# Transposing three quarters of the second branch's attention output by DMA, as 16 bit halves, instead of on TensorE

## The chip, the cores and the metric

The kernel runs on one core of one Trainium2 chip. The metric is the device time of one execution in microseconds (us); the median of three runs of the kernel before is 1930.79 us (1929.85 to 1930.82). A core has five engines that run side by side, each with its own queue in program order: TensorE (PE, with its weight loads as PEld), VectorE (DVE), ScalarE (ACT), GpSimd (POOL) and SyncE (SP). SP computes nothing here; nearly all DMAs are issued from its queue, in order, and 16 DMA engines then move the bytes.

## The reference

One encoder block on a 2048 x 1024 input, in single precision. What matters here, cut to its core:

```python
h = rms_norm(x, norm_gain)
qa, ka, va, qb, kb, vb, ga, gb, mg = split(h @ w_in)
ya = banded_attention(rms(qa), rms(ka), va, 128, ...) * silu(ga)
for g, (window, dilation) in enumerate(((128, 1), (512, 4), (2048, 16))):
    o, l = dilated_group(rms(qb[g]), rms(kb[g]), vb[g], window, dilation, ...)
yb = sum(softmax(lses) * outs) * silu(gb)
x = x + (sigmoid(mg_a) * (ya @ w_branch_a) + sigmoid(mg_b) * (yb @ w_branch_b)) @ w_out
```

The first branch (`ya`, A) and the second (`yb`, B) each give a 2048 x 512 output. The projections that use them want it with features on the partitions, the attention makes it with tokens on the partitions, so all of it has to be transposed once.

## The kernel before

**Stages.** First the input is normalised, transposed and split into two half precision tiles `XH` and `XL` (high and low part). Then comes the attention phase, from about 82 to 1250 us of the span. After it come the remaining gates by a Strassen-like scheme (`fps` tiles, line 1576), the branch projections (1885) and the output projection (1957).

**The attention phase** works through 14 units, in the order A0, B(0,1), A1, B(0,2), B(0,0), B(1,1), B(1,2), B(1,0), B(2,1), ... B(3,0); in B(p,g), p is one of four pairs of heads and g the dilation group. A unit has 8 pairs, and a pair projects two blocks of 128 tokens to queries, keys and values (`Pair`, line 677; matmuls into `pj`, line 694). ACT, DVE and POOL then normalise them and split them into halves (`rw`, `spl`; lines 708 to 776), and a DMA transpose turns each block's queries and keys (`kq<-spl`, line 784). For each block of queries an `Item` (line 788) has logits on TensorE (`s<-kq`, 844), maxima, exponentials and a split on DVE and ACT (859 to 876), a DMA transpose of the probabilities (`pt<-p`, 882) and values on TensorE (`pv<-vt,pt`, 893). Within a pair of heads the unit of group 0 is last: there `b_merge_q` (1024) merges the three groups with what was stored of the other two (`zz<-zd`, 902) into the tile `ya` (1062, 1063), 256 tokens at a time.

**The transpose in question.** Every 512 tokens, when a `ya` tile of 128 tokens x (4 blocks x 128 features) is full, a `YPart(chunk, q, y)` (932) is planned. Chunks 0 to 3 are branch A, chunk 4 + p is head pair p of branch B, and q counts the four 512 token pieces. For branch B it does this: four single precision transposes of 128 x 128 on TensorE into one PSUM bank (`turn`, 957), one copy by ACT to SBUF (`gate`, 962, tile `yo` out of a ring of three), and a store to DRAM (`store`, 974, `ytd<-yo`). The later stages load `ytd`.

**What sets the order.** The attention phase is recorded with a manual schedule: `at(t, f)` puts a step at a logical time on one list, where one unit of t is one pair (some 9.7 us while the group 0 units run), and the steps are written out in the order of t. So each engine's queue, SP's with it, holds its instructions in exactly that order, and a queue whose first instruction waits holds back all behind it. `Y_PART` (69) gives the offsets of a YPart's steps, `B_MERGE` those of the merge, `NORM` (62) those of the normalisation up to the `kq` transpose. The weights of the next unit are loaded 384 KB at a time at the start of a unit (`wraw`, 175), since the offsets are logical, and the last two pairs' `kq` transposes of a unit are issued when the next unit has begun.

Of the kernel before, what the change touches and what calls it, by code (L numbers as in the profile page):

```python
# [21 lines left out]
F32 = mybir.dt.float32  # L22
F16 = mybir.dt.float16
I32 = mybir.dt.int32
AF = mybir.ActivationFunctionType
OP = mybir.AluOpType
AX = mybir.AxisListType
# [38 lines left out]
OUT = 0.007  # L66
A_MERGE = (0.085, 0.224, 0.51, 0.59, 1.398, 0.699)
B_MERGE = (-0.037, 0.133, 0.333, 0.507, 0.665, 0.991)
Y_PART = (-0.02, 0.571, 0.797, 0.981, 1.031)
GATE = (-0.062, 0.084, 0.255)  # L70
W_STEP = (0.1, 0.6, 1.9, 0.445, 4.186, 0.117, 0.301)
# [34 lines left out]
def block_kernel(tc, x, w_units, w_gate, w_mrg, w_out, w_bra, w_brk, gain, qkg, sink, bias_a, bias_b, b_merge, out):  # L106
    nc = tc.nc
    V = nc.vector
    A = nc.scalar
# [14 lines left out]
    def ucol():  # L124

        ucount[0] += 1
        return ubuf[:, ucount[0] - 1:ucount[0]]
# [15 lines left out]
    def pow2(mx, name):  # L143
# [3 lines left out]
        p = sm.tile([128, 1], F32, name="pw_p")  # L147
        V.tensor_scalar(p[:].bitcast(I32), m[:].bitcast(I32), 0x7F800000, None, OP.bitwise_and)
        r = sm.tile([128, 1], F32, name="pw_r")
# [39 lines left out]
    def norm_pow(ps):  # L189
# [5 lines left out]
        p = sm.tile([128, 1], F32, name="pw_p")  # L195
        V.tensor_scalar(p[:].bitcast(I32), m[:].bitcast(I32), -0.5, float(0x5F3759DF), OP.mult, OP.add)
        V.tensor_scalar(p[:].bitcast(I32), p[:].bitcast(I32), 0x7F800000, None, OP.bitwise_and)
        s = ucol()
# [5 lines left out]
    def w_square(u, i):  # L204
# [4 lines left out]
        c = slice(2 * i, 2 * i + 2)  # L209
        A.activation(wtiles[u][2][:, c, :n], raw[:, c, :n], AF.Square, accum_out=wtiles[u][3][:, i:i + 1])  # L210

# [11 lines left out]
    def w_hi(u, i):  # L223
        n = 384 if u < NU else 256
        raw, s, inv, wh, wl = wtiles[u]
        c = slice(2 * i, 2 * i + 2)
        A.activation(wh[:, c, :n], raw[:, c, :n], AF.Copy, scale=s[:])

# [20 lines left out]
    def rs_guess(a, n):  # L249

        y = sm.tile([128, 10], F32, name="rs_y")
        A.activation(y[:, :n], a, AF.Ln)
        A.activation(y[:, :n], y[:, :n], AF.Exp, scale=-0.5)
        return y[:, :n]
# [25 lines left out]
    gp = gps.enter_context(tc.tile_pool(name="gp", bufs=1, side="right"))  # L280
# [33 lines left out]
    def g_square(c):  # L314
        gh = sp0.tile([128, NCH, 128], F16, name="gh", bufs=2)
        gl = sp0.tile([128, NCH, 128], F16, name="gl", bufs=2)
        sq = sm.tile([128, 1], F32, name="gsq")
        A.activation(gh[:], gw[c][0], AF.Square, accum_out=sq[:])
        gw[c] += [gh, gl, sq]
# [11 lines left out]
    def g_hi(c):  # L331
        gh, gl, ih, raw, s = gw[c]
        A.activation(gh[:], raw, AF.Copy, scale=s[:])

# [45 lines left out]
    def at(t, f, *args):  # L380
        seq[0] += 1
        heapq.heappush(heap, (t, seq[0], f, args))
# [8 lines left out]
    def chain(steps):  # L391

        steps = sorted(steps, key=lambda e: e[0])
        done = [0]

        def go(k):
            if done[0] < k or steps[k][1](*steps[k][2:]) is False:
                at(now[0] + .04, go, k)
            else:
                done[0] = k + 1  # L400

        for k, e in enumerate(steps):
            at(e[0], go, k)
# [141 lines left out]
    n = 0  # L545
    for k in X_LD:
        for i in range(4 if k == "u" else 1):
            f, args = {"g": (gain_load, ()), "u": (w_load, (0, (i,)))}.get(k, (x_load, (k,)))
            if k in ("w0", "w1"):
                f, args = g_load, (int(k[1]),)  # L550
# [126 lines left out]
    class Pair:  # L677
# [21 lines left out]
        def plan(self, e):  # L699

            for i in range(2):
                for d, f in zip(EVAC, (self.evac_qk, self.v_hi, self.v_lo)):
                    at(e[i] + d, f, i)
            steps = (self.square, self.stats, self.newton, self.scale, self.gain, self.hi, self.lo, self.swap, self.turn)
            for d, f in zip(NORM, steps):
                at(e[1] + d, f)
# [225 lines left out]
    class YPart:  # L932
# [5 lines left out]
        def load(self):  # L938
# [3 lines left out]
            assert ("gt", self.chunk, self.q) in done  # L942
            nc.sync.dma_start(out=self.o[:], in_=gtd[self.chunk][:, 512 * self.q:512 * self.q + 512])

        def plan(self, t):
            steps = [(t + d, f) for d, f in zip(Y_PART, (self.load, self.turn, self.gate, self.top, self.store))]
            if self.q == 3 and self.chunk < 2:
                steps += [(t + Y_PART[3] + d, f) for d, f in zip(Y_MAX, (self.max1, self.max2, self.max3))]
            chain(steps)
# [74 lines left out]
    def b_merge_q(t, un, zz, q):  # L1024
# [33 lines left out]
        def sums():  # L1058
# [5 lines left out]
            if q % 2:  # L1064
                YPart(4 + j, q // 2, un.y).plan(t + B_MERGE[5])

        for d, f in zip(B_MERGE, (collect, exponents, exps, factors, products, sums)):
            at(t + d, f)
# [135 lines left out]
    for u in range(NU + 1):  # L1204
        t = 8 * u
# [8 lines left out]
    for k in range(8):  # L1214
        u = 3 + k
        t = 8 * u
# [10 lines left out]
    t = 0  # L1227
# [644 lines left out]
    class Branch(Seven):  # L1872
        n, mm_us = 7, MM1
# [65 lines left out]
    class Out(Seven):  # L1939
        n, mm_us = 7, MM  # L1940
# [52 lines left out]
    for s in range(8):  # L1993
        p = pos[0]
# [92 lines left out]
```

## Time and profile before

| | |
|---|---|
| median of 3 runs | 1930.79 us |
| the profiled execution | 1929.74 us, span 1927.9 us |
| granted TensorE clock | 0.998 of full speed |
| DMA transposes `pt<-p` and `kq<-spl` | 256 and 224 |
| TensorE transposes on line 957 | 128, 64 of them for branch B |

The span is what lies between the first and the last recorded instruction; the 1.8 us beside it are start and end. In a timeline row the columns are start, duration (both us), engine (a q marks its queue, which issues DMAs or waits), line, operation, tiles written<-read, form and count, and in brackets the idle time ahead of it with what ended it. Matmuls are pipelined, so the distance between two starts, not the duration, is what one costs the queue.

### The profile page before, as it was taken

The numbers are of one execution on the slowest core, as the hardware profiler recorded it, in microseconds if no ns is written. First come the engines' busy times: TensorE is split into PE (matmuls) and PEld (weight loads), VectorE is DVE, ScalarE is ACT, GpSimd is POOL, SyncE is SP. The second block draws the span as 40 slices with busy tenths as digits, with TensorE's granted clock in tenths as the row PEclk, the third lists the DMA queues.
The fourth block names the chain that finished last, engine by engine and source line by source line (L and its number), as shares of the span: only waits on it lengthen the run. The fifth ranks groups of instructions, "written<-read, shape, count | busy, mean of one in ns | idle before, by whom it ended". The sixth has DMA issues, their size and how long they took to land.

```text
span 1927.9 us, 51082 instructions
## 1 busy us (share of the span) xinstructions
PE 1875.8 (97%) x19242; PEld 1439.0 (75%) x19242; DVE 1505.6 (78%) x3835; ACT 1251.6 (65%) x3015; POOL 578.0 (30%) x1363
## 2 busy tenths in 40 slices
PE   6999999999999999999999999899999999999998
PEld 4568987789999899989999898444444446776774
DVE  7679878986887888888888888658778754987885
ACT  8477768886777777777766766565575775433441
POOL 1034343443453435543455445200000001232121
PEclk9999999999999999999999999999999999999999
DMA  6259998987878679878888677666565568854541
GB/s 254 82 103 194 169 187 138 195 167 156 169 147 181 151 147 201 149 159 173 147 171 161 133 151 152 169 243 206 181 203 172 171 195 269 275 158 123 148 147 68
DMA packets 643447, 326.21 MB, mean 169 GB/s; under 512 B 459264, under 2 KB 598144, under 8 KB 640768
## 3 DMA queue, kind: packets, MB, share of 16 engines
q1 hardware_dynamic: 643056, 322.70, 71.6%
q8 instruction: 150, 2.46, 0.6%
q14 instruction: 97, 0.79, 0.1%
q10 hardware_dynamic: 144, 0.26, 0.0%
HBM read 139.08 MB, written 73.66 MB: 110 GB/s over the span
## 4 chain that ended last, share of the span: by engine, by line
PE 87%; DMA 5%; DVE 4%; ACT 2%; issue 1%; POOL 0%; SPq 0%; DVEq 0%; POOLq 0%
PE pj L694 42%; PE fps L1576 17%; PE fps L1957 7%; PE fps L1885 6%; PE s L844 5%; PE pv L893 4%; DMA pt<-p 2%; PE pj L349 2%; PE pj L301 1%; DMA kq<-spl 1%; PE fps L301 1%; DVE y L1734 1%; PE pt L957 1%; PE s L479 0%; DMA bigl<-sd 0%
## 5 line engine op out<-in xcount | busy, mean ns | idle before, releaser
L694 PE MATMUL pj<-wl,XH 128*128 128x128 f16 (+2 forms) x2816 | 715.2, 268 | 0.0
L694 PE MATMUL pj<-wh,XL 128*128 128x128 f16 (+2 forms) x2816 | 711.6, 269 | 0.0
L694 PE MATMUL pj<-wh,XH 128*128 128x128 f16 (+2 forms) x2816 | 708.6, 268 | 0.0
L694 PEld LDWEIGHTS <-XH 128*128 128x128 f16 x5632 | 575.0, 112 | 54.1
L694 PEld LDWEIGHTS <-XL 128*128 128x128 f16 x2816 | 315.8, 112 | 23.8
L859 DVE CUSTOM_DVE_ANT_0 pr<-s,b,ubuf 128x256 f32<-128x256 f32 (+3 forms) x512 | 219.0, 465 | 44.9 <-PE s L844 42.2
L876 DVE SCALAR_TENSOR_TENSOR p<-pr,p 128x512 f16<-128x512 f32 (+2 forms) x256 | 195.8, 765 | 50.6 <-ACT p L872 48.9
L761 POOL TENSOR_TENSOR rw<-rw,g 128x128 f32<-128x128 f32 (+1 forms) x224 | 149.1, 685 | 202.7 <-DVE rw L754 182.4
L1895 POOL TENSOR_TENSOR g<-g,t 128x512 f32<-128x512 f32 x32 | 48.4, 1514 | 536.6 <-DMA g<-mgd 391.8
L1576 PEld LDWEIGHTS <-wh 128*128 128x128 f16 x1064 | 104.3, 99 | 131.9 <-issue 6.7
L712 ACT ACTIVATE rw<-pj 128x256 f32<-128x256 f32 (+1 forms) x224 | 87.5, 390 | 137.8 <-PE pj L694 137.2
L776 POOL COPY spl<-spl 128x256 f16<-128x256 f16 (+1 forms) x224 | 96.5, 460 | 247.7 <-DVE spl L771 247.7
L872 ACT ACTIVATE p<-pr 128x512 f16<-128x512 f32 (+2 forms) x256 | 157.7, 616 | 15.1 <-DMA pt<-p 10.5
L1885 PE MATMUL fps<-y,bigh 128*128 128x128 f16 x1792 | 153.7, 219 | 2.8 <-DVE r L1818 2.8
L844 PE MATMUL s<-kq 128*128 128x128 f16 (+1 forms) x1856 | 148.4, 218 | 6.7 <-DMA kq<-spl 5.8
L1957 PE MATMUL fps<-WO,mf 128*128 128x512 f16 x672 | 150.3, 379 | 2.4 <-DVE xr L1964 2.4
L1885 PE MATMUL fps<-y,bigl 128*128 128x128 f16 x896 | 151.8, 219 | 0.0
L844 PEld LDWEIGHTS <-kq 128*128 128x128 f16 x2016 | 131.1, 98 | 22.9 <-issue 7.7
L1885 PEld LDWEIGHTS <-bigh 128*128 128x128 f16 x1792 | 139.1, 98 | 10.5 <-issue 3.2
L893 PE MATMUL pv<-vt,pt 128*128 128x65 f16 (+1 forms) x2784 | 131.6, 193 | 8.8 <-DMA pt<-p 8.0
L893 PEld LDWEIGHTS <-pt 128*128 128x128 f16 x3024 | 119.2, 97 | 25.0 <-DMA pt<-p 12.5
L767 ACT ACTIVATE spl<-rw 128x512 f16<-128x512 f32 (+1 forms) x112 | 72.1, 643 | 79.5 <-POOL vt L723 74.0
(250 smaller groups left out, 3823.5 us busy)
## 6 DMA issues: line engine op xcount, KB each, us to landing
wraw<-in_w_units_dram SPq DMA_DIRECT2D x56, 384.0 KB, 4.7
g<-mgd SPq DMA_DIRECT2D x64, 256.0 KB, 5.0
wraw<-in_w_mrg_dram SPq DMA_DIRECT2D x45, 256.0 KB, 5.0
mgd<-t SPq DMA_DIRECT2D x43, 256.0 KB, 3.0
zd<-z SPq DMA_DIRECT2D x128, 66.0 KB, 2.0
zz<-zd SPq DMA_DIRECT2D x64, 132.0 KB, 3.4
xt<-in_x_dram SPq DMA_DIRECT2D x16, 512.0 KB, 7.9
ytd<-yo SPq DMA_DIRECT2D x32, 256.0 KB, 3.3
```

The lines of the kernel that those rows point to most:

```text
L694: out.append(lambda lhs=lhs, rhs=rhs, ch=ch, a=a, b=b, k=k: T.matmul(ps[:, a:b], lhsT=lhs[:, ch, :], rhs=rhs[:, ch, a:b], start=(k == 0), ...
L712: A.activation(self.rw[:, n * i:n * i + n], self.ps[i][:, :n], AF.Copy)
L761: G.tensor_tensor(q[:, i, :un.nq, :], q[:, i, :un.nq, :], g, OP.mult)
L776: G.tensor_copy(sp[:, i, nh:, :, :], sp[:, i, nq:nh, ::-1, :])
L844: T.matmul(self.sv[j][:, o:o + k1 - k0], lhsT=q[:, h, :], rhs=kt[:, un.nq + kh + v * un.nk, k0:k1], start=(v == 0), stop=(v == 1))
L859: V.tensor_tensor_reduce(out=self.pv[:, j, self.p0:self.p0 + W], in0=self.sv[j], in1=un.bias[:, self.h0 + j, self.b0:self.b0 + W], scale=I ...
L872: A.activation(self.sp[:, :128 * n], self.pr, AF.Copy, scale=PSC)
L876: V.scalar_tensor_tensor(self.sp[:, 128 * n:], self.pr, PSC, self.sp[:, :128 * n], OP.mult, OP.subtract)
L893: T.matmul(self.po[:, j, :w], lhsT=p[:, n * j + s, :], rhs=un.v[key][:, vh, c0:c0 + w], start=(k == 0 and s == 0), stop=(k == 2 and s == n ...
L1576: T.matmul(b[k][:], lhsT=w[:, i, ch, :], rhs=xform(PROD[i][0], lo, ch, q), start=(i < 3 and n == 0), stop=(n == 11), skip_group_check=True)
L1885: out.append(lambda p=p, c=c, wl=wl, yl=yl, n=n: T.matmul(ps[:, 128 * p:128 * p + 128], lhsT=w[wl][:, i, c, p, :], rhs=y[:, yl, c, :], sta ...
L1957: out.append(lambda p=p, ml=ml, wl=wl, k=k: T.matmul(ps[:], lhsT=m[:, ml, p, :], rhs=WO[:, i, wl, p, :], start=(fresh and k == 0), stop=(k ...
```

## The change

12 of branch B's 16 YParts plus (7,0), that is chunks 4, 5, 6 and piece 0 of chunk 7, no longer go through TensorE. ACT copies `ya` into a `yo` tile seen as 1,024 16 bit numbers per partition, first all low halves and then all high halves (`halves`). One DMA transpose from SP turns the eight 128 x 128 blocks of 16 bit numbers into a second `yo` tile (`turn_halves`). ACT puts the halves back together in a third (`join`), and the store is as before. Pieces 1 to 3 of chunk 7 stay on TensorE.

```diff
+Y_BITS, Y_PE = (0.1, 0.3, 1.0, 1.5), ((7, 1), (7, 2), (7, 3))
...
+        def halves(self):
+            self.s = gp.tile([128, 512], F32, name="yo", bufs=3)[:].bitcast(U16)
+            A.activation(self.s.rearrange("p (t b c) -> p t b c", t=2, b=4),
+                         self.y[:].bitcast(U16).rearrange("p b (c t) -> p t b c", t=2), AF.Copy)
+
+        def turn_halves(self):
+            self.t = gp.tile([128, 512], F32, name="yo", bufs=3)[:].bitcast(U16)
+            nc.sync.dma_start_transpose(out=self.t.rearrange("p (a b) -> p a b", b=128), in_=self.s)
+
+        def join(self):
+            self.o = gp.tile([128, 512], F32, name="yo", bufs=3)
+            A.activation(self.o[:].bitcast(U16).rearrange("p (n t) -> p t n", t=2), self.t.rearrange("p (t n) -> p t n", t=2), AF.Copy)
+
         def plan(self, t):
+            if self.chunk > 3 and (self.chunk, self.q) not in Y_PE:
+                for d, f in zip(Y_BITS, (self.halves, self.turn_halves, self.join, self.store)):
+                    at(t + d, f)
+                return
             steps = [(t + d, f) for d, f in zip(Y_PART, (self.load, self.turn, self.gate, self.top, self.store))]
```

The line numbers of the changed kernel are larger by 2 ahead of this place and by 19 behind it. How the order changes is shown at the first YPart of B(0,0). SP's queue there, before, from the last probabilities of one step to the keys of the unit's eighth pair (`b` is a bias load):

```order
L882 DMA_TRANSPOSE pt_9597<-p_9534 128x8x128
L668 DMA b_9610<-in_bias_b_dram 128x512
L175 DMA wraw<-in_w_units_dram 128x768 x2
L902 DMA zz<-zd_82 128x2x132 x2
L784 DMA_TRANSPOSE kq<-spl 128x6x128 x2
L882 DMA_TRANSPOSE pt_9729<-p_9655 128x8x128
L175 DMA wraw<-in_w_units_dram 128x768 x2
L974 DMA ytd<-yo 128x512
L882 DMA_TRANSPOSE pt_9842<-p_9777 128x8x128
L902 DMA zz<-zd_82 128x2x132 x2
L784 DMA_TRANSPOSE kq<-spl 128x6x128 x2
```

The same stretch of SP's queue with the change:

```order
L884 DMA_TRANSPOSE pt_9598<-p_9534 128x8x128
L670 DMA b_9611<-in_bias_b_dram 128x512
L954 DMA_TRANSPOSE yo<-yo 128x8x128
L177 DMA wraw<-in_w_units_dram 128x768 x2
L904 DMA zz<-zd_82 128x2x132 x2
L786 DMA_TRANSPOSE kq<-spl 128x6x128 x2
L884 DMA_TRANSPOSE pt_9727<-p_9658 128x8x128
L177 DMA wraw<-in_w_units_dram 128x768 x2
L884 DMA_TRANSPOSE pt_9840<-p_9774 128x8x128
L904 DMA zz<-zd_82 128x2x132 x2
L993 DMA ytd<-yo 128x512
L786 DMA_TRANSPOSE kq<-spl 128x6x128 x2
```

The new DMA transpose (954) stands ahead of the first weight loads, and so ahead of the keys of both the seventh and the eighth pair; the store of the result (974, now 993) has moved behind one `pt` and one `zz` group, but is still ahead of the eighth pair's keys. ACT's queue at the same place, before, where the values of the piece's last block are copied (`zz<-pv`):

```order
L872 ACTIVATE p_9534<-pr 128x512
L917 ACTIVATE zz<-pv 128x2x65
L767 ACTIVATE spl<-rw 128x2x4x64
L712 ACTIVATE rw<-pj 128x256
L724 ACTIVATE vt<-pj 128x2x64
L737 ACTIVATE spl<-rw 128x512
```

With the change:

```order
L874 ACTIVATE p_9534<-pr 128x512
L919 ACTIVATE zz<-pv 128x2x65
L949 ACTIVATE yo<-ya 128x1024
L769 ACTIVATE spl<-rw 128x2x4x64
L714 ACTIVATE rw<-pj 128x256
L726 ACTIVATE vt<-pj 128x2x64
L739 ACTIVATE spl<-rw 128x512
```

`halves` (949) now stands directly ahead of the split of the seventh pair's queries and keys (767, now 769). One pair later ACT's queue reads, before:

```order
L712 ACTIVATE rw<-pj 128x256
L962 ACTIVATE yo<-pt 128x512
L724 ACTIVATE vw<-pj 128x2x64
L867 ACTIVATE pr<-pr,nmB 128x256 x2
L872 ACTIVATE p_9777<-pr 128x512
L917 ACTIVATE zz<-pv 128x2x65
L767 ACTIVATE spl<-rw 128x2x4x64
```

With the change:

```order
L714 ACTIVATE rw<-pj 128x256
L726 ACTIVATE vw<-pj 128x2x64
L869 ACTIVATE pr<-pr,nmB 128x256 x2
L874 ACTIVATE p_9774<-pr 128x512
L958 ACTIVATE yo<-yo 128x2x512
L919 ACTIVATE zz<-pv 128x2x65
L769 ACTIVATE spl<-rw 128x2x4x64
```

The copy out of PSUM (962) is gone, and `join` (958) stands ahead of a copy of values and of the split of the eighth pair's queries and keys. DVE's and POOL's queues are the same instruction for instruction, and TensorE's lacks the four transposes in 13 places.

More of the change, by code (lines that the diff above doesn't have):

```diff
@@ L24 @@
 I32 = mybir.dt.int32
+U16 = mybir.dt.uint16
 AF = mybir.ActivationFunctionType
```

## The prediction

> **What bounds the kernel now.** I read the page first, then the stretches with branch B's pieces, then TensorE's waits and the chain of waits, then SP's and TensorE's timelines. The page's busy times, and three stretches around units B(0,0), B(1,0) and B(2,0) (us, then busy time of PE, PEld, DVE, ACT, POOL, the granted clock, the DMA engines' share, GB/s):
>
> ```profile
> PE 1875.8 (97%) x19242; PEld 1439.0 (75%) x19242; DVE 1505.6 (78%) x3835; ACT 1251.6 (65%) x3015; POOL 578.0 (30%) x1363
> ...
> 500.00:590.00 90.00, 88.62 (x1266) 87.14 (x1264) 78.50 (x256) 64.42 (x177) 49.24 (x129) 1.00 0.90 173
> 725.00:815.00 90.00, 90.00 (x1287) 88.76 (x1285) 78.67 (x259) 66.05 (x183) 50.12 (x132) 1.00 0.94 178
> 950.00:1040.00 90.00, 88.51 (x1256) 87.21 (x1254) 79.15 (x259) 63.73 (x176) 50.27 (x130) 1.00 0.84 158
> ```
>
> TensorE sets the time: it runs through, so what leaves its queue is won. But where the change adds DMA work the DMA engines are 84 to 94% busy, and the little that TensorE loses is waiting for a DMA. The view of waits, and four pieces of the chain of waits (start, length):
>
> ```profile
> PE s L844 <- DMA kq<-spl: 5.8, 4, 2.9
> ...
> 501.03 6.67 DMA kq<-spl
> 532.32 5.47 DMA kq<-spl
> 969.72 7.27 DMA kq<-spl
> 1203.22 5.10 DMA kq<-spl
> ```
>
> All four are key transposes of a unit of group 0, which is where the pieces fall; at these places TensorE already waits for a DMA that SP issued. The question is what a further DMA does there.
>
> **What is removed.** TensorE's timeline where the first piece was turned, and the line's own row (durations least/median/most):
>
> ```profile
> 520.84 0.60 PE L957 MATMUL pt<-idf,ya 128*128 128x128 f32 x4
> 521.28 0.27 PE L694 MATMUL pj<-wh,XL 128*128 128x256 f16 x1
> ...
> L957 PE MATMUL pt<-idf,ya x128: 272/273/280, 167.6 to 1237.5; 128*128 128x128 f32 x128
> ```
>
> The next matmul starts 0.44 us after the first of four transposes, so a piece costs 0.44 us of TensorE, and 13 pieces 5.7 us. That is the most there is to win, 0.30%. The Trainium skill ("TensorE: Matmul & The Clock Gate", PE-mode transpose) puts a 128 x 128 transpose in a kernel's context at about 275 ns. The row's 273 ns agrees as a duration, but the queue moves on after 0.11; were 275 ns what each costs, 52 would give 14.3 us.
>
> **What is added, where it is exposed.** SP's queue, in order, at the first piece of B(0,0):
>
> ```profile
> 518.88 0.57 SPq L668 DMA_DIRECT2D b<-in_bias_b_dram  x1
> 519.50 0.90 SPq L175 DMA_DIRECT2D wraw<-in_w_units_dram  x2
> 520.50 1.62 SPq L902 DMA_DIRECT2D zz<-zd  x2
> 522.22 3.25 SPq L784 DMA_TRANSPOSE kq<-spl  x2
> 525.58 1.25 SPq L882 DMA_TRANSPOSE pt<-p  x1
> 526.88 1.05 SPq L175 DMA_DIRECT2D wraw<-in_w_units_dram  x2
> 528.03 0.38 SPq L974 DMA_DIRECT2D ytd<-yo  x1
> 528.52 1.50 SPq L882 DMA_TRANSPOSE pt<-p  x1
> 530.11 2.12 SPq L902 DMA_DIRECT2D zz<-zd  x2
> 532.32 2.16 SPq L784 DMA_TRANSPOSE kq<-spl  x1
> ```
>
> From 518.88 on SP issues without a pause for 14 us. The new transpose comes between `b` and `wraw`, at 519.5. It is of the shape of `pt<-p` here (8 blocks of 128 x 128 of 16 bits), which holds SP for 1.25 us (the row at 525.58). So the seventh pair's keys leave at 523.5 instead of 522.2 and the eighth's at 533.6 instead of 532.3; the store that moves stays ahead of the eighth pair's keys. How much room is there? The landing of the seventh pair's first transpose after its issue, and when TensorE takes it; then the same for B(1,0), seventh and eighth pair:
>
> ```profile
> DMA to landing us min/median/max: 5.0/5.0/5.0
> ...
> 527.14 0.61 PE L844 MATMUL s<-kq 128*128 128x128 f16 x8
> ...
> 746.07 2.97 SPq L784 DMA_TRANSPOSE kq<-spl  x2
> ...
> DMA to landing us min/median/max: 4.6/4.6/4.6
> ...
> 751.73 0.61 PE L844 MATMUL s<-kq 128*128 128x128 f16 x8
> ...
> 756.01 2.55 SPq L784 DMA_TRANSPOSE kq<-spl  x2
> ...
> 761.27 0.61 PE L844 MATMUL s<-kq 128*128 128x128 f16 x8
> ```
>
> In B(0,0) the seventh pair's keys land at 522.2 + 5.0 = 527.2, as TensorE takes them: no room; the eighth's land at 532.32 + 5.47 = 537.8 and are waited for. In B(1,0) the seventh has 751.8 - 750.7 = 1.2 us, the eighth (landing 5.0 too) 761.4 - 761.0 = 0.4. In B(2,0) the seventh (969.72) and in B(3,0) the eighth (1203.22) are on the chain, without room.
>
> So each unit's first piece delays the keys by d. Bounds of d: 1.25 us if only SP's time counts, as the DMA engines have a pause just ahead (first row below, share 0.35) and the new bytes could move while the weights are not yet issued. At the other end SP's time and the transfer's own come one behind the other:
>
> ```profile
> 516.00:518.00 2.00, 2.00 (x25) 1.84 (x23) 1.83 (x7) 0.82 (x3) 1.02 (x3) 1.00 0.35 30
> ...
> q1 hardware_dynamic: 643056, 322.70, 71.6%
> ```
>
> 71.6% of 1927.9 us over 643,056 packets is 2.1 ns of all 16 engines each, and 1,024 rows of 256 bytes are at that mean 2.2 us; d = 3.4. Below 1.25 nothing excludes d = 0 if the queue of bytes, not of issues, sets the landing. I take 1.5, near the issue row, since the pauses behind SP were none and those of the DMA engines some.
>
> TensorE is then late at the eighth pair by: B(0,0) 1.5; B(1,0) 1.5 - 0.4 = 1.1; B(2,0) 1.5; B(3,0) 1.1, since there SP stood idle for about 0.4 us ahead of the second of these rows:
>
> ```profile
> 1199.66 0.41 SPq L974 DMA_DIRECT2D ytd<-yo  x1
> 1200.55 1.40 SPq L882 DMA_TRANSPOSE pt<-p  x1
> ```
>
> Sum 5.2 us. These are places where a DMA ends the wait, so the 0.44 us that leaves TensorE just ahead of them (the first piece of each of the four units) is lost in them.
>
> **What is added, where it is hidden.** The other nine pieces (three each of B(0,0), B(1,0) and B(2,0)) fall into the next unit's first five pairs. Their keys have room; the tightest that I found behind B(0,0):
>
> ```profile
> 581.11 2.80 SPq L784 DMA_TRANSPOSE kq<-spl  x2
> ...
> 591.25 0.28 PE L844 MATMUL s<-kq,kq 128*128 128x128 f16 x2
> ```
>
> The second of the two leaves at 582.4, lands 5.0 later and is taken at 591.2: 3.8 us, more than d's upper end. So nine times 0.44 = 3.9 us are won.
>
> ACT gets two copies of 1,024 elements for one of 512:
>
> ```profile
> L438 ACT ACTIVATE jk<-xt x16: 1039/1054/1085, 6.3 to 42.9; 128x1024 f16<-128x1024 f32 x16
> ...
> 517.01 0.63 ACT L767 ACTIVATE spl<-rw 128x512 f16<-128x512 f32 x1 [0.81 <-POOL vt L723]
> ...
> 519.49 0.74 POOL L776 COPY spl<-spl 128x256 f16<-128x256 f16 x2 [2.47 <-DVE spl L771]
> ...
> 525.86 0.63 ACT L872 ACTIVATE p<-pr 128x512 f16<-128x512 f32 x1
> ...
> 528.77 0.39 ACT L712 ACTIVATE rw<-pj 128x256 f32<-128x256 f32 x1 [0.88 <-PE pj L694]
> ```
>
> By the first row 1.05 us each. I cost them at nothing: `halves` takes the 0.81 us of idle time ahead of 517.01 and moves that split by under 1 us, and the keys made of it were ready at 520.2, 2.0 us before SP took them. `join` follows the split of 525.86, ends at about 527.5, and ACT idles before 528.77. The transposed halves, issued at 519.5, land 5 us later, before `join` needs them. Without that cover each would hold the keys by 1.05 us.
>
> A rule speaks against the whole change: the Trainium skill ("VectorE: DVE Perf Modes", The three transpose paths and its rules) gives TensorE 390 ns and DMA 1309 ns for a 128 x 128 block and says to use TensorE where PSUM will do. By that, eight blocks would take 10.5 us, `join` would wait some 3.5 us, and ACT would hold back the next keys. Landings of 5 us for whole transposes in this stretch speak against that size.
>
> **Sum.** 5.2 lost, 3.9 won: +1.3 us. The profiled execution (1929.74, span 1927.9 and 1.8 around it) would be 1931.0; the median of the runs lies 1.05 above it, so 1932.1, in round numbers 1932 us. With d = 1.25 it is 1931.1; with d = 3.4, (3.4 + 3.0 + 3.4 + 3.0) - 3.9 = +8.9 and 1939.7.
>
> **Rivals.** *All hidden*: the bytes, not SP's issues, set when keys land, the new bytes fill the pause at 516 to 520, and d is about 0. Then 3.9 to 5.7 us are won: 1925 to 1927. For it: landings of 5 to 7 us are transfers queueing, not issues. Against it: SP without a pause for 14 us. *In series, slower*: at the seventh pair's keys, SP's 1.25 us and the transfer's up to 2.2 us add up; from d = 2.2 on the loss is 3.9 us net (4 x 2.2 - 0.8 - 3.9), so it gives 1935 to 1940. For it: the 7.27 us landing at 969.72, where two weight loads stand just ahead and the new transpose joins them. Against it: the transfer can start while SP issues the next. *The transposes cost TensorE their duration*: 52 times 0.273 = 14.2 won, 5.2 lost, 1921.8; the row at 521.28 is against it. It is the case that the Trainium skill's page on TensorE gives if its 275 ns are the queue's time. *Nothing changes*: excluded, since the order shows the transposes gone.
>
> **Chances.** Won and lost nearly even: 0.44; its own range, d from 0.7 to 2.1, is 1929 to 1934.5. In series: 0.38. All hidden: 0.16. Duration: 0.02. 0.2% of 1930.8 is 3.9 us, about what a measurement of this kernel can tell from no change. The hidden case (3.9 to 5.7 won) and the duration case lie beyond it on one side, the series case (3.9 to 8.9 lost) on the other: faster 0.18, same 0.44, slower 0.38. The range for 8 in 10 reaches into both, from 1926 to 1938.5; about 0.1 each way is left out.
>
> **What would show it.** Right: gaps of `s<-kq` behind a DMA in all four units, the seventh pair's keys leaving SP 1.2 us or more later against the probabilities ahead of them, no new gap at the other nine pieces, TensorE with 52 transposes fewer and no idle time for `yo`. Wrong: keys that land no later (then all hidden), landings behind the new transpose longer by over a us (in series), or idle time of ACT behind `yo` (the cost I put at nothing).

## The result: 0.33% slower

| | before | changed |
|---|---|---|
| median | 1930.79 us (5 runs, 1925.87 to 1931.32) | 1936.71 us (5 runs, 1934.06 to 1937.34) |
| ratio, with its 95% interval | 1 | 1.0033 (1.0022 to 1.0043) |
| the profiled execution | 1929.74 us, span 1927.9 | 1934.06 us, span 1932.1 |

The two medians lie 5.9 us apart, and the ratio makes +6.4 us (4.2 to 8.3). All of the interval is beyond 0.2%, so the kernel got slower, by more than the 1.2 us forecast and less than the range allowed. Below, a ratio is turned into us by the median of before that the same runs gave.

The page's busy times and the three stretches of the windows view, for the changed kernel (columns as before):

```profile
PE 1871.7 (97%) x19190; PEld 1435.1 (74%) x19190; DVE 1506.2 (78%) x3835; ACT 1271.5 (66%) x3028; POOL 585.5 (30%) x1363
...
500.00:590.00 90.00, 88.04 (x1252) 86.46 (x1250) 76.81 (x252) 69.06 (x176) 50.59 (x126) 1.00 0.95 176
725.00:815.00 90.00, 87.82 (x1255) 86.31 (x1252) 77.24 (x253) 69.31 (x178) 50.95 (x126) 1.00 0.94 181
950.00:1040.00 90.00, 86.87 (x1224) 84.84 (x1223) 77.91 (x252) 67.35 (x173) 50.78 (x125) 0.98 0.90 164
```

TensorE has its 52 transposes fewer and is busy 4.1 us less. Yet in the second stretch it stands still for 2.2 us, where it never stopped before, and in the third for 3.1 in place of 1.5. What it waits for is the keys, as the view of waits and TensorE's timeline at all eight of these waits show (idle time and what ended it in the brackets):

```profile
PE s L846 <- DMA kq<-spl: 13.6, 8, 3.3
...
526.76 0.49 PE L846 MATMUL s<-kq 128*128 128x128 f16 x6 [1.09 <-DMA kq<-spl]
537.21 0.49 PE L846 MATMUL s<-kq 128*128 128x128 f16 x6 [0.75 <-DMA kq<-spl]
595.39 0.49 PE L846 MATMUL s<-kq 128*128 128x128 f16 x6 [1.20 <-DMA kq<-spl]
732.22 0.49 PE L846 MATMUL s<-kq 128*128 128x128 f16 x6 [0.32 <-DMA kq<-spl]
753.32 0.50 PE L846 MATMUL s<-kq 128*128 128x128 f16 x6 [1.86 <-DMA kq<-spl]
978.52 0.69 PE L846 MATMUL s<-kq 128*128 128x128 f16 x5 [3.07 <-DMA kq<-spl]
1201.91 0.50 PE L846 MATMUL s<-kq 128*128 128x128 f16 x6 [2.06 <-DMA kq<-spl]
1212.13 0.50 PE L846 MATMUL s<-kq 128*128 128x128 f16 x6 [3.26 <-DMA kq<-spl]
```

The four of before:

```profile
507.74 0.49 PE L844 MATMUL s<-kq 128*128 128x128 f16 x6 [0.51 <-DMA kq<-spl]
537.84 0.49 PE L844 MATMUL s<-kq 128*128 128x128 f16 x6 [0.88 <-DMA kq<-spl]
977.03 0.49 PE L844 MATMUL s<-kq 128*128 128x128 f16 x6 [1.49 <-DMA kq<-spl]
1208.36 0.80 PE L844 MATMUL s<-kq 128*128 128x128 f16 x6 [2.92 <-DMA kq<-spl]
```

5.8 us of waits for keys became 13.6. Six of the eight are the seventh and eighth pairs of the four group 0 units, behind the first pieces. The one at 595.39 lies in B(1,1), behind the last piece of B(0,0), at a place that the prediction had called hidden. The 0.32 us at 732.22 come in B(1,0) ahead of its first piece; a run without any new DMA has 0.5 us at the same place (run 11 below), so I don't count them to the change. SP's queue at the first piece of B(0,0):

```profile
517.56 0.57 SPq L670 DMA_DIRECT2D b<-in_bias_b_dram  x1
518.23 2.14 SPq L954 DMA_TRANSPOSE yo<-yo  x1
520.42 1.04 SPq L177 DMA_DIRECT2D wraw<-in_w_units_dram  x2
521.56 0.89 SPq L904 DMA_DIRECT2D zz<-zd  x2
522.56 2.66 SPq L786 DMA_TRANSPOSE kq<-spl  x2
```

From the probabilities ahead of `b` to the first keys SP now takes 6.3 us (it issued them at 516.27) where it took 4.6 before (517.59 to 522.22), and it still runs without a pause. The new transpose holds SP for 2.1 us here. In B(1,0), B(2,0) and B(3,0) the same distance grew by 1.5, 1.5 and 2.5 us.

A second reading follows the k-th of the 8,448 `pj` matmuls, which both kernels have, from one trace to the other. Behind twelve of the pieces the changed kernel's start moves ahead by 0.44 us at once; the thirteenth stands behind the last of these matmuls. It falls back by 1.25 us at 527.6 of before, 1.35 at 596.3, 0.48 at 732.7, 2.02 at 752.2 and 3.0 from 977.4 on. Of these 3.0, 1.8 come at once, and 1.2 over the next fourteen matmuls: behind the wait of 3.07 us TensorE's granted clock is 0.50 from 979 to 981 us, which is what makes the third stretch's 0.98.

### The profile page after: what moved, and what is told of

It reads as the page before. It is cut to its first block, busy times and chain, and to the rows that moved or that the text cites. A ratio compares the mean times of both kernels' runs of the same rounds, so it can differ in the third digit from the quotient of the medians.

```text
span 1932.1 us, 51009 instructions
## 1 busy us (share of the span) xinstructions
PE 1871.7 (97%) x19190; PEld 1435.1 (74%) x19190; DVE 1506.2 (78%) x3835; ACT 1271.5 (66%) x3028; POOL 585.5 (30%) x1363
## 4 chain that ended last, share of the span: by engine, by line
PE 83%; DMA 7%; DVE 5%; ACT 2%; issue 2%; SPq 1%; POOL 1%; DVEq 0%; POOLq 0%
PE pj L696 39%; PE fps L1595 17%; PE fps L1976 7%; PE fps L1904 6%; PE s L846 5%; PE pv L895 4%; DMA kq<-spl 3%; DMA pt<-p 2%; PE pj L351 2%; PE pj L303 1%; PE fps L303 1%; DVE y L1753 1%; PE s L481 0%; DVE pr L861 0%; DVE qss L744 0%
## 5 line engine op out<-in xcount | busy, mean ns | idle before, releaser
L846 PE MATMUL s<-kq 128*128 128x128 f16 (+1 forms) x1856 | 150.1, 219 | 14.6 <-DMA kq<-spl 13.6
L1904 PEld LDWEIGHTS <-bigh 128*128 128x128 f16 x1792 | 139.0, 98 | 10.5 <-issue 3.1
L1595 PE MATMUL fps<-bigh,wh 128*128 128x512 f16 x304 | 116.1, 382 | 6.2 <-ACT r L1604 2.8
```

What stands on the lines that cost most here:

```text
L846: T.matmul(self.sv[j][:, o:o + k1 - k0], lhsT=q[:, h, :], rhs=kt[:, un.nq + kh + v * un.nk, k0:k1], start=(v == 0), stop=(v == 1))
L1595: T.matmul(b[k][:], lhsT=w[:, i, ch, :], rhs=xform(PROD[i][0], lo, ch, q), start=(i < 3 and n == 0), stop=(n == 11), skip_group_check=True)
L1904: out.append(lambda p=p, c=c, wl=wl, yl=yl, n=n: T.matmul(ps[:, 128 * p:128 * p + 128], lhsT=w[wl][:, i, c, p, :], rhs=y[:, yl, c, :], sta ...
```

## The experiments

Twelve kernels were run, each beside the kernel before. All times but the profiles' are medians of 5 to 12 runs; "us" is the ratio less 1, times the median of before's executions beside them (1930.40, 1929.77, 1928.99 and 1929.67 for runs 1 to 4, 5 to 8, 9 to 11, and 12).

| run | what differs | ratio (95% interval) | us (interval) |
|---|---|---|---|
| 1 | change, first pieces left on TensorE | 0.9995 (0.9983 to 1.0006) | -1.0 (-3.3 to +1.2) |
| 2 | change, only the four first pieces | 1.0027 (1.0017 to 1.0037) | +5.2 (+3.3 to +7.1) |
| 3 | before + 4 DMA transposes | 1.0026 (1.0015 to 1.0038) | +5.0 (+2.9 to +7.3) |
| 4 | before + 13 pairs of ACT copies | 1.0003 (0.9994 to 1.0011) | +0.6 (-1.2 to +2.1) |
| 5 | before + 3 small copies, 4 times | 1.0047 (1.0032 to 1.0062) | +9.1 (+6.2 to +12.0) |
| 6 | before + 4 transposes from ACT's queue | 1.0098 (1.0084 to 1.0111) | +18.9 (+16.2 to +21.4) |
| 7 | change, first pieces' transposes moved | 0.9998 (0.9987 to 1.0009) | -0.4 (-2.5 to +1.7) |
| 8 | run 1, `join` later | 0.9995 (0.9984 to 1.0006) | -1.0 (-3.1 to +1.2) |
| 9 | before + 2 small copies, 4 times | 1.0036 (1.0022 to 1.0051) | +6.9 (+4.2 to +9.8) |
| 10 | before + the other 9 DMA transposes | 1.0020 (1.0009 to 1.0032) | +3.9 (+1.7 to +6.2) |
| 11 | before - 13 pieces' transposes | 0.9971 (0.9959 to 0.9983) | -5.6 (-7.9 to -3.3) |
| 12 | before + 2 small copies, 9 times | 1.0013 (1.0001 to 1.0025) | +2.5 (+0.2 to +4.8) |

### Runs 1 and 2: which pieces lose

```diff
-Y_PE = ((7, 1), (7, 2), (7, 3))
+Y_PE = ((4, 0), (5, 0), (6, 0), (7, 0), (7, 1), (7, 2), (7, 3))          # run 1
+Y_PE = tuple((c, q) for c in (4, 5, 6, 7) for q in (1, 2, 3))            # run 2
```

> Only the first piece of each of the four units goes back to TensorE; the other nine stay on the DMA path. Theory (the loss is made at the first pieces, where the new transpose stands on SP ahead of the weights and the keys): the nine pieces win 9 x 0.44 = 3.9 us, of which the new wait of 1.2 us behind B(0,0)'s last piece stays, so 2.5 to 4 us below before, 1927 to 1928.5 us. Rival (the loss goes with the number of pieces: ACT's copies and the DMA engines' bytes): 9/13 of the 5.9 us between the medians, so 4 us above before, 1935 us.

> The complement: only the first piece of each of the four units goes by DMA, the other nine are turned by TensorE as before. Theory (first pieces): the waits for keys that the changed kernel shows in these four units grow by about 7.8 us, 4 x 0.44 = 1.8 us are saved, so about 6 us above before, 1936 to 1938 us. Rival (loss by number of pieces): 4/13 of 5.9 = 1.8 us above before, 1932.6 us.

Run 2 with its four pieces loses 5.2 us, a little under the 6 expected and most of what the change loses; a loss by number of pieces would be 1.8, outside its interval. Run 1 loses nothing, so that rival (+4) is out as well. But run 1 doesn't win the 3.9 us of the prediction either: its interval ends at 3.3 below before. The four first pieces are the place of the loss, and the nine others about break even.

### Runs 3 and 4: SP's transpose or ACT's copies

```diff
+        def extra(self):                                                  # run 3; q == 0, t + 0.3
+            self.t = gp.tile([128, 512], F32, name="yo", bufs=3)[:].bitcast(U16)
+            nc.sync.dma_start_transpose(out=self.t.rearrange("p (a b) -> p a b", b=128), in_=self.y[:].rearrange("p b c -> p (b c)").bitcast(U16))
...
-                for d, f in zip(Y_BITS, (self.halves, self.turn_halves, self.join, self.store)):
-                    at(t + d, f)
-                return
+                at(t + Y_BITS[0], self.halves)                            # run 4
+                at(t + Y_BITS[2], self.join)
```

> The kernel before, with nothing taken from TensorE and nothing added on ACT; at the first piece of each of the four units SP issues one more DMA transpose of eight 128x128 blocks of 16 bits, at the place where the change has it, of the piece's own bytes into a buffer that nobody reads. Theory (SP's slot and the transfer): keys late as in the changed kernel, 5 to 8 us above before, 1936 to 1939 us. Rival (ACT's two copies make the keys late): under 1 us above before, 1931 to 1932 us.

> The kernel before, with ACT's two copies of 1,024 elements added for all thirteen pieces (the second reads what the first wrote) and no DMA transpose added; TensorE still turns the pieces and ACT still evicts them. Theory (ACT has room): 0 to 1.5 us above before, 1931 to 1932.5 us. Rival (ACT's copies make the splits and so the keys late): 4 us or more above before, from 1935 us.

Four transposes whose output nobody reads cost 5.0 us without any work on ACT or any gain on TensorE; thirteen pairs of copies cost 0.6 us, with an interval that holds zero. (In run 4 the second copy has no transpose to wait for.) So the first pieces lose by what SP issues, not by ACT. In run 3's trace the wait for keys in B(1,0), where the kernel before has none, is there again, and SP's rows ahead of it are those of the change:

```profile
744.25 0.57 SPq L670 DMA_DIRECT2D b<-in_bias_b_dram  x1
744.88 1.23 SPq L962 DMA_TRANSPOSE yo<-ya  x1
746.15 1.07 SPq L177 DMA_DIRECT2D wraw<-in_w_units_dram  x2
747.32 0.89 SPq L904 DMA_DIRECT2D zz<-zd  x2
748.31 2.71 SPq L786 DMA_TRANSPOSE kq<-spl  x2
...
753.98 0.49 PE L846 MATMUL s<-kq 128*128 128x128 f16 x6 [1.09 <-DMA kq<-spl]
```

### Runs 5 and 9: the slot on SP or the bytes

```diff
-            nc.sync.dma_start_transpose(...)
+            for k in range(3):                                            # run 5; range(2) in run 9
+                nc.sync.dma_start(out=self.t[16 * k:16 * k + 16, 0:256], in_=self.y[16 * k:16 * k + 16, 0, :].bitcast(U16))
```

> As the run with the transpose alone, but at each of the four places SP issues three small copies (16 rows of 512 bytes each, 24 KB together against 256 KB) in place of the one DMA transpose. At some 0.42 us each they hold SP for about the same 1.25 us and move hardly any bytes. Theory (SP's slot sets d): the keys leave as late, and the time is 4 to 5 us above before, 1934.5 to 1935.5 us. Rival (the transfer's bytes ahead of the weights and the keys set d): within 1.5 us of before, 1930 to 1932 us.

> As the run with three small copies, with two: SP then issues for 2 x 0.63 = 1.26 us more at each of the four places, which is just the DMA transpose's own 1.25 us, with 16 KB in place of 256 KB. If the slot alone counts: as the transpose alone, 4 to 6 us above before, 1934 to 1936 us. If its bytes count too, this run comes out lower than the transpose alone by 2 us or more, 1931 to 1932.5 us.

The same rows of run 9, in the same unit:

```profile
742.58 0.57 SPq L670 DMA_DIRECT2D b<-in_bias_b_dram  x1
743.20 1.23 SPq L963 DMA_DIRECT2D yo<-ya  x2
744.48 1.05 SPq L177 DMA_DIRECT2D wraw<-in_w_units_dram  x2
745.64 0.89 SPq L904 DMA_DIRECT2D zz<-zd  x2
746.63 2.71 SPq L786 DMA_TRANSPOSE kq<-spl  x2
...
752.43 0.49 PE L846 MATMUL s<-kq 128*128 128x128 f16 x6 [1.48 <-DMA kq<-spl]
```

Two copies of 8 KB hold SP for 1.23 us, just what the transpose of 256 KB holds it for in run 3; from there to the keys it is 3.43 us in both, and TensorE waits for them in both. The price is +6.9 us against +5.0, with intervals that overlap: a sixteenth of the bytes, and no lower. Run 5's three copies took 1.86 us a place, more than the 1.25 expected, and cost more too:

```profile
745.74 1.86 SPq L963 DMA_DIRECT2D yo<-ya  x3
```

So at the first pieces the time on SP's queue is enough for the whole loss. Per us that SP issues more, over the four places, it costs 4.1 us in run 3 (5.0 / 1.23), 5.6 in run 9 and 4.9 in run 5, 1.0 to 1.4 us at each place. The Trainium skill ("DMA: Bandwidth & Descriptors", on issuing engines that are not separate DMA queues) calls the issuing sequencer's time usually small relative to the DMA itself; here it is what is paid for, and the transfer is not.

### Run 6: from another queue

```diff
-            nc.sync.dma_start_transpose(...)
+            nc.scalar.dma_start_transpose(...)
```

> The converse: the same four extra DMA transposes at the same places, issued from ACT's queue, so that SP issues nothing more. Rival (bytes): 4 to 5 us above before, 1934.5 to 1935.5 us. Theory (SP's slot): SP's order and times are those of before, so within 1.5 us of before, 1930 to 1932 us, unless ACT's issue makes a split late; then ACT shows 1.2 us more of it at the four places.

18.9 us, far above both. A new wait took over, so the run says nothing on slot against bytes. SP's waits, and its rows at the first piece of B(0,0):

```profile
SPq L786 <- DMA yo<-ya: 23.6, 4, 7.1
...
522.76 1.02 SPq L904 DMA_DIRECT2D zz<-zd  x2
529.71 2.54 SPq L786 DMA_TRANSPOSE kq<-spl  x2
```

SP stands still from 523.8 to 529.7, since the program as built makes the next transpose on SP wait until the one from ACT's queue has landed, four times. The Trainium skill ("DMA: Bandwidth & Descriptors", the part on two transposing streams in flight at once) says that transposes of two queues can corrupt each other, so that the later must wait for the earlier's completion. The wait is in this trace; no run here shows the corruption.

### Runs 7 and 8: other places

```diff
+Y_FIRST = (0.1, 1.65, 2.2, 2.6)                                           # run 7
-                for d, f in zip(Y_BITS, ...
+                for d, f in zip(Y_FIRST if self.q == 0 else Y_BITS, ...
...
-Y_BITS = (0.1, 0.3, 1.0, 1.5)
+Y_BITS = (0.1, 0.3, 1.4, 1.75)                                            # run 8, with run 1's Y_PE
```

> The changed kernel, with the four first pieces' DMA transposes moved on SP from ahead of the weights to behind the eighth pair's keys (the joining copy and the store go later too). Theory (what is lost is lost by the place on SP): the keys of the seventh and eighth pairs land as before, no new wait in these pairs; the thirteen pieces then win what the nine did and up to 1.8 us more, so 1926 to 1930 us, unless the next unit's first keys, 4 to 5 us behind in B(0,0), are made late. Rival (a DMA transpose costs wherever it stands): as the changed kernel, 1935 to 1937 us.

> The run with the first pieces on TensorE, and the joining copy of the other nine moved on ACT behind the next split (1.4 pairs after the piece in place of 1.0), the store with it. Theory (what is left of the loss there is the joining copy, which waits on ACT for its DMA transpose ahead of a split): no wait for keys behind B(0,0)'s last piece, and the full 3.9 us, 1926.5 to 1928 us. Rival (nothing is won by it, the difference is within runs): as that run, 1928 to 1930 us.

Run 7 has all thirteen transposes of the change, and its time is that of before: at the first pieces the place on SP makes the loss, not the transpose (`join` and the store go later with it, which run 8 shows to be worth nothing at the other nine). SP's rows in B(0,0) show the new place; the longest wait for keys in its profile is 1.0 us, where the changed kernel's is 3.3:

```profile
PE s L847 <- DMA kq<-spl: 5.0, 6, 1.0
...
531.36 4.13 SPq L787 DMA_TRANSPOSE kq<-spl  x2
535.55 1.31 SPq L955 DMA_TRANSPOSE yo<-yo  x1
536.96 3.49 SPq L885 DMA_TRANSPOSE pt<-p  x2
```

Run 8 gives what run 1 gave, not the 3.9 us expected; the later `join` shows no gain. Runs 1, 7 and 8 all beat the changed kernel, and none can be told from the kernel before.

### Runs 10 to 12: why the nine don't win

```diff
+            if self.chunk > 3 and self.q and (self.chunk, self.q) not in Y_PE:
+                at(t + Y_BITS[1], self.extra)                             # run 10: transpose, run 12: two small copies
...
+            if self.chunk > 3 and (self.chunk, self.q) not in Y_PE:       # run 11, in turn
+                self.ps = self.y[:].rearrange("p b c -> p (b c)")
+                return
```

> The kernel before, with nothing taken away; at the other nine pieces SP issues the DMA transpose of the piece's own bytes into a buffer that nobody reads. Theory of the prediction (these nine are hidden): no change, 1929.5 to 1931.5 us. Rival (they make keys late where less room is left, which is why the run with the first pieces on TensorE won under the 3.9 us): 2 to 3 us above before, 1932 to 1933.5 us.

> The kernel before without the transposes of the thirteen pieces, and nothing in their place: ACT copies the untransposed piece, so the rows handed on aren't the reference's. Theory (0.44 us a piece, and the first piece's lost in the wait for keys behind it): 9 x 0.44 = 3.9 to 13 x 0.44 = 5.7 us below before, 1924.5 to 1927 us. Rival (a transpose costs TensorE its whole duration of 273 ns): 14 us below, 1916 us. Second rival (what TensorE wins it waits for elsewhere): under 2 us below, 1928.5 us or more.

> As the run with the nine transposes alone, with two small copies (16 KB, 1.26 us of SP) in place of each: nine slots on SP and hardly any bytes. If the slot is what costs here too: as the nine transposes, 2 to 6 us above before. If it is their bytes, which keep the DMA engines busy behind them: within 1.5 us of before, which the room for the keys of the next unit's fifth and sixth pair would show as near to that of before.

Run 11 gives the price of what is removed: 5.6 us, which is 13 x 0.44 = 5.7, and neither 14 nor under 2. Its interval (3.3 to 7.9) holds nine times 0.44 too, but in its trace the waits for keys are 5.0 us in all against 5.8 before, so there the first pieces' 0.44 isn't lost in them. Run 10 takes 3.9 back for the nine transposes alone, and 9 x 0.44 = 3.9 won less 3.9 lost is the nought that run 1 measured within its interval. What the nine take from the room of the keys can be followed at the keys of B(1,1)'s sixth pair. Before, SP issues them at 588.92, they land 2.8 us later, and TensorE takes them at 595.86:

```profile
588.92 2.54 SPq L784 DMA_TRANSPOSE kq<-spl  x2
...
595.86 0.61 PE L844 MATMUL s<-kq 128*128 128x128 f16 x8
```

They have 4.2 us of room. In the changed kernel TensorE stood idle 1.20 us for them at 595.39 (above). The chain of waits there (start, length), and ACT's timeline:

```profile
579.47 6.74 DMA yo<-yo
590.82 4.52 DMA kq<-spl
...
586.23 1.39 ACT L958 ACTIVATE yo<-yo 128x1024 uint16<-128x1024 uint16 x1 [1.45 <-DMA yo<-yo]
...
588.67 0.62 ACT L769 ACTIVATE spl<-rw 128x512 f16<-128x512 f32 x1
```

The piece's transpose takes 6.74 us to land, `join` waits for it on ACT, and the split of the sixth pair (588.67) stands behind `join`. The keys leave SP 1.9 us later, at 590.82, and then land in 4.5 us in place of 2.8. `join` alone isn't what holds them, though: SP issues without a pause from 578.2 until it comes to them. In run 10, which has nothing more on ACT, the keys leave SP at 590.41, take 4.3 us, and TensorE takes them at 594.97:

```profile
579.56 2.82 SPq L962 DMA_TRANSPOSE yo<-ya  x1
...
590.41 3.16 SPq L786 DMA_TRANSPOSE kq<-spl  x2
...
594.97 0.61 PE L846 MATMUL s<-kq 128*128 128x128 f16 x8
```

0.3 us of room is left of 4.2. In run 12, with small copies, SP gets on sooner, and the keys, issued at 589.35 and landing in 2.8 us, keep 3.4 us:

```profile
580.09 1.34 SPq L963 DMA_DIRECT2D yo<-ya  x2
...
589.35 2.60 SPq L786 DMA_TRANSPOSE kq<-spl  x2
...
595.50 0.61 PE L846 MATMUL s<-kq 128*128 128x128 f16 x8
```

At this place, then, the transpose costs more room than two small copies do: it held SP for 2.8 us, not 1.25, and what was issued behind it landed later. In the medians runs 10 and 12 (+3.9 and +2.5) can't be told apart, so how the 3.9 us divide between slots and bytes stays open.

The same happens behind the fourth piece of B(1,0), a unit that the prediction didn't search. Before, the keys of B(2,1)'s sixth pair leave SP at 812.48, land at 816.2 and are taken at 819.41: 3.3 us of room. In run 10 the transpose holds SP for 3.3 us, and 0.8 us of room is left; in run 7 TensorE waits there for 1.0 us, and for 0.5 at B(1,1)'s sixth pair.

That room is lost is shown; where the 3.9 us are paid is not. In run 10's own profile TensorE waits at neither of these places, and it is that run's shortest execution. The waits at the two places make at most 1.5 us in any profile here, so the greater part of the 3.9 us stays unlocated.

## Why the prediction was right or wrong

**What bounds the kernel: right.** The loss shows as idle time of TensorE, and in the attention phase the waits that grew were all for `kq`. The expected sign, waits of `s<-kq` behind a DMA in all four group 0 units, is there, and the seventh pair's keys leave SP 1.7, 1.5, 1.5 and 2.5 us later against the probabilities, where 1.2 or more was forecast.

**What is removed: right.** 0.44 us a piece by the trace, 5.6 (3.3 to 7.9) for thirteen by run 11. The rival by which a transpose costs its 273 ns is out.

**The first pieces: right in mechanism and in size.** 5.2 us was forecast for the four together, their own 0.44 counted as lost, and run 2 measured 5.2 (3.3 to 7.1). The working behind it was a little off in both directions: in run 11's trace the 0.44 isn't lost, and on the whole d was larger than the 1.5 taken. In the changed kernel's trace the waits of the four units grew by 1.0, 1.9, 1.6 and 2.4 us (the rows of after less those of before), 6.8 together before rounding, where 1.5, 1.1, 1.5 and 1.1 were forecast; 6.8 less four times 0.44 is 5.0. That forecast and run 2 agree to the tenth is luck. That SP's slot sets d was taken from the rows of SP without a pause; runs 3 and 9 bear it out.

**In series, slower: its time came true, its cause did not.** 1936.7 us lies in its 1935 to 1940, but the transfer's bytes don't add at the seventh pair's keys: run 9 moves a sixteenth of them and costs no less. Its sign, landings longer by over a us, came in B(1,0), where the seventh pair's first keys landed in 5.8 us in place of 4.6; but with run 9's small copies they took 5.8 us as well. (Its sum, 4 x 2.2 - 0.8 - 3.9, is 4.1 and not 3.9, which changes nothing.)

**What is added where it is hidden: wrong, and this is the step that failed.** The nine other pieces were to win 3.9 us, since "the tightest that I found behind B(0,0)" was 3.8 us of room against a d of 3.4 at most. Together they break even (run 1), and their transposes alone cost 3.9 us (run 10). Two things were wrong in it. d was bounded with a slot on SP of 1.25 us, read at a first piece; behind the fourth pieces of B(0,0) and B(1,0) the new transpose holds SP for 3.2 and 2.6 us (median of the thirteen 1.3), and there it took 3.9 us of room from the keys of B(1,1) with nothing added on ACT (run 10). And one unit was searched where the claim was on three: the sixth pair of B(2,1) had 3.3 us of room, less than the 3.4 that d was given at most. Which waits add up to the loss of the nine stays open. The new transposes' row and their landing times:

```profile
L954 SPq DMA_TRANSPOSE yo<-yo x13: 1232/1288/3171, 518.2 to 1194.0; - x13
...
DMA to landing us min/median/max: 3.1/3.4/6.7
```

The second row answers the estimate of 10.5 us for eight blocks, which the prediction worked out from the rate in the Trainium skill ("VectorE: DVE Perf Modes", The three transpose paths): they landed in 3.4 us (median), 6.7 at most. That page's rule to use TensorE held here, but by SP's time and not by that rate.

**ACT at nothing: right in size, though its sign appeared.** ACT does idle for the new copies, 13 times ahead of `halves` until `ya` is ready, by its view of waits (us in total, times, longest), and 2.5 us ahead of `join`:

```profile
ACT yo L949 <- DVE ya L1082: 13.2, 13, 2.1
...
  DMA yo<-yo: 2.5, 2
```

Run 4 puts the copies at 0.6 us (-1.2 to +2.1), and moving `join` (run 8) shows no gain. At the place followed above `join` does delay a split, but SP was busy until it came to the keys made of it.

**The sum.** 5.2 lost and 3.9 won were to leave +1.3. The parts as measured, run 2 plus run 1, leave 5.2 - 1.0 = +4.2, at the lower end of the change's own interval of +4.2 to +8.3. In the single profile the span grew by 4.2: 7.8 more of waits for keys less 5.7 won make 2.1, and 1.4 of the other 2.1 is a longer wait of `fps` for `xr` in the output stage (3.8 us against 2.4), which the change doesn't touch and which I take for scatter: it is 2.4 to 3.8 us in the profiles of the twelve runs. The last 0.7 us stay open. So the case held likeliest, no difference beyond 0.2%, did not come; the slower one, given 0.38, did. The time lies within the stated 1926 to 1938.5 us only because that range took in part of the series case, whose cause is not the one that was found.

## What to carry to other kernels

Moving work off the bound engine won what its queue distance says (0.44 us for four transposes), not its duration, so what decides is the queue that takes it over: count that queue's issue time at the places where something behind it has no room, and put the new instruction behind those, not ahead. Room is to be read for every place where the work lands, and the delay set against it has to be taken from that place too, since the same DMA held its queue for 1.2 us at one place and 3.2 at another. A step that is replaced by one on a full queue can be tested in halves: take the old away alone, and add the new alone.

## What the runs showed that I had not expected

- Executions of one kernel scatter more than the three runs of before (1929.85 to 1930.82) let see: 34 of them, those beside runs 1 to 4, lay between 1924.29 and 1933.67 us. A single profile can so mislead by some 6 us: run 10's was 1927.76 us, its fastest, with a median of 1933.54. The verdicts here stand on medians, and profiles only show where.
- The scatter goes with TensorE's granted clock. Of the 24 executions of before beside runs 9 to 11, the five with a mean clock of 0.999 took 1925.2 to 1927.1 us, the two with 0.995 took 1931.4 and 1934.9. In the attention phase of the profiles the clock falls to a half for 3.4 us at a time, behind some of the long waits for keys: behind 3.07 us at 978.5 in the changed kernel, behind 3.33 us at 732.4 in run 1, but not behind 3.26 us at 1212.1 in the changed kernel. So a wait can cost more than its length. Run 10's executions had 0.9967 on average against 0.9973 for before's; whether that is part of its price or chance isn't shown.
- A copy of 8 KB holds SP for 0.6 us, a transpose of 256 KB for 1.23: making a DMA 32 times smaller only halved its hold on the queue.
- A second queue for DMA transposes isn't free: each one from ACT's queue made SP's next one wait, 23.6 us for four.
